# SSD chunk states: kept contiguous per chunk, with the recurrence as a chain of small operations

## The chip, the cores and the metric

The kernel runs on one core of a Trainium2 chip. The metric is the device time of one execution in microseconds; several runs are timed and their median is given.

## What is computed

One inference step of an encoder layer for a prompt of 1024 tokens and a sample of 32 tokens, width 1024, all in f32. After a conditioned RMSNorm an input projection (1024 to 4624 columns) feeds two groups: an RG-LRU group and an SSD group (16 heads of 64, two groups of B and C, state 128). Their outputs go through one output projection and a final RMSNorm. The change lies in the SSD group alone. Of the reference, cut:

```python
def ssd_scan(x, dA, Bm, Cm, s0, q):
    ...
    y_diag = jnp.einsum('bclgn,bcsgn,bgkcls,bcsgkp->bclgkp', Cm, Bm, Lm, x)   # inside a chunk
    states = jnp.einsum('bcsgn,bgkcs,bcsgkp->bcgkpn', Bm, decay_states, x)    # what a chunk adds
    ...
    new_states = ...    # state after chunk c = decay of chunk c * state before it + what it adds
    start_states, final = new_states[:, :-1], new_states[:, -1]
    y_off = jnp.einsum('bclgn,bcgkpn,bgkcl->bclgkp', Cm, start_states, jnp.exp(A_cs))
    return y_diag + y_off, final
```

(The reference writes the two products of `CB` and `y_diag` apart; they are drawn together here.) The kernel uses chunks of 128 tokens: chunks 0 to 7 are the prompt, whose state starts at zero, and chunk 8 is the sample, whose state starts from a given one. The final states of both are outputs.

## The kernel before

Channels lie on partitions, tokens on the free axis. The input projection takes a unit of 128 output channels at a time: `load_unit` fetches 512 KB of weights, ScalarE rounds them to the matmul's reduced f32 format (`whi`, L95), VectorE forms the remainder (`wlo`, L97), and TensorE does three products per piece (`pj`, L219 to L221) for three blocks of tokens (384, 384 and 290 columns).

The SSD stage is a loop of eight steps j (L685 to L712), two heads per step. A step has these parts:

- `ssd_tokens` (L558): transposes the inputs and scales them by dt, into `xdt` and `xw`.
- `ssd_decay` (L543): loads broadcast rows of decays `M` and `E` and scans `M` (L551).
- `ssd_states` (L573): for each of nine chunks one matmul adds up the chunk's contribution, [128 states, 128 = 2 heads x 64], into PSUM (`pd`, also called `dS` in the trace, L588): four chunks in one bank, four in the next, chunk 8 in a third. ScalarE copies the banks into the SBUF tile `dS` (L591), of shape [128, 128, 10]: for each of the 128 columns ten slots lie side by side, 0 to 7 for the chunks of the prompt, 8 for the sample's starting state (loaded into `st0`, copied by GpSimd, L579), 9 for the sample's chunk. ScalarE also spreads the decays of the chunks into a tile `dk` of the same shape (L580), with zeros in slots 0 and 8. One VectorE instruction then scans over all 1280 elements (L592): state = decay * state + contribution, where the zeros start the recurrence anew. GpSimd copies slots 7 and 9 into `sfin` (L595, L596), which is stored.
- `ssd_diag` (L600): the inside of each chunk, `yd` (L610), two matmuls per chunk, then `y` (L613).
- `ssd_off` (L617): for chunks 1 to 8 a matmul `yo` (L625) with the state before the chunk as weights, `dS[:, :, e]`, and `CT` as the moving operand; VectorE scales it by `E` (L628) and adds it to `y` (L629).

Between these, each step multiplies two units of the input projection and one of the conditioning (`ada_s`, `ada_row`, `ada_c`). The small products share four PSUM banks in turn, in the order in which the program asks for them (tag `g`); the projection has the other four. So the third piece of `yd` (chunk 8) takes over the bank in which the contributions of chunks 4 to 7 stood. `dS` has one buffer, so the state's parts of step j + 1 wait for the `yo` of step j.

In this stage the order of instructions on each engine is set by a list scheduler, which may put later projection matmuls between these parts. Each engine runs its own list in order; all DMAs are issued from SP's queue.

Of the kernel before, what the change touches and what calls it, by code (L numbers as in the profile page):

```python
# [8 lines left out]
F32 = mybir.dt.float32  # L9
F32R = mybir.dt.float32r  # L10
AF = mybir.ActivationFunctionType
OP = mybir.AluOpType
# [15 lines left out]

# columns of the packed per-channel parameters
P_NG, P_BADA, P_LCW, P_LCB = 0, 8, 32, 64  # L30
# [5 lines left out]

# The start. XLOAD: the order of the loads: x a piece of x, s a unit of w_ada (the scale's, then the
# shift's), w w_dt, B and C the first two tiles of the input projection's B columns. XP: pieces of x per
# block of tokens; SR: buffers for units of w_ada; POOL_K: the tiles of block 0 that GpSimd scales.
# PROG: the order on TensorE: r and R sum up a block's squares and spread its 1/rms, a and s multiply a  # L40
# unit of the scale's or the shift's, c turns finished rows into columns, d is a block of dt, p and q a
# k-tile of the two B tiles, W keeps the array's clock up where nothing is there to multiply.
WARM = 8
XP = (4, 2, 2)
SR = 6
POOL_K = (3, 5, 6)
XLOAD = "xxxxsxsCsBssswxsxsxssssssss"
PROG = ("WWWWWWWWWaWWWWWWraWRWcWaWWWWWWcWWWWqpaWWWaqcaqWp"
        "aWcqppapqcrqqRppdqprpqsqpRqppssqpqqpsssppqssdq")
# [8 lines left out]
def encoder_step(ctx: ExitStack, tc: tile.TileContext, a, o):  # L58
    nc = tc.nc
# [9 lines left out]
    dma = nc.sync.dma_start  # L69
# [3 lines left out]

    # ------------------------------------------------------------------ constants
    cT = const.tile([128, KT, 2], F32, name="cT")
# [9 lines left out]
    sel = const.tile([128, 32], F32, name="sel")  # L85

    # ------------------------------------------------------------------ weight units
    def fetch_unit(src):
        raw = wpool.tile([128, KT, 128], F32, name="wraw", tag="wraw", bufs=3)
        dma(raw, src)  # L90
        return raw
# [8 lines left out]
    def load_unit(src):  # L100
        return split_unit(fetch_unit(src))

    # ------------------------------------------------------------------ conditioning
    sc = const.tile([128, KT, 32], F32, name="sc")
# [3 lines left out]

    # four column tiles of the array share a unit's contraction; sel adds up their rows
    def ada_unit(raw, row, copy=nc.vector.tensor_copy):  # L110
        ps = pbank([128, 128], "ada_s")
        for kk in range(KT):
            q = slice(32 * (kk % 4), 32 * (kk % 4) + 32)
            nc.tensor.matmul(ps[q, :], lhsT=sc[:, kk, :], rhs=raw[:, kk, :], start=(kk < 4), stop=(kk >= 4))
        copy(row, ps)
# [6 lines left out]

    # 1 / rms of each token, tokens on partitions, from the sums over channel tiles of the squares; and
    # its spread over all partitions, tokens on the free axis
    def chunks(n):
        return [(c, t, min(128, n - t)) for c, t in enumerate(range(0, n, 128))]
# [26 lines left out]

    # ------------------------------------------------------------------ normalised input
    # channels on partitions; XB: a block's columns of x and its chunks of tokens
    XB = ((0, 384), (384, 384), (768, 288))
# [56 lines left out]

    # ------------------------------------------------------------------ input projection
    def mm_part(out, w, b, kk):
# [32 lines left out]

    # start: conditioning, h, dt and the first B tiles; what needs the shift comes last
    wdt = st.tile([128, KT, 16], F32, name="wdt")  # L250
# [7 lines left out]
    shift = st.tile([128, KT, 2], F32, name="shift")  # L258
    bk_b0, bk_b1 = {}, {}

    # rows 0..15 and 16..31: the products with the head and the tail of w_dt
    def dt_block(b):
# [9 lines left out]
    with tc.manual_schedule(engines={mybir.EngineType.SP, mybir.EngineType.PE}):  # L272
# [12 lines left out]

        # into the bank that the first of the k-tiles of block 1 overwrites
        def warm(n):
            for i in range(n):
                nc.tensor.matmul(bk_b0[1][:, 0:128], lhsT=ones[:, 0:128], rhs=ones[:, 0:128], start=True, stop=True)
# [47 lines left out]
        loads = list(XLOAD)  # L337
        for c in PROG:
            while loads and load_next():
                pass  # L340
            n = cnt[c]
            cnt[c] += 1
            b, k = divmod(n, KT)
# [15 lines left out]
            else:  # L359
                i = "pq".index(c)  # L360
# [8 lines left out]
        pd = dt_block(2)  # L369
# [5 lines left out]

    # tokens of each chunk on partitions, [chunk, head] on the free axis
    dtv = const.tile([128, 9, 16], F32, name="dtv")
    nc.gpsimd.memset(dtv, -1.0e4)
    pt = pbank([128, 9, 16], "dtT")
    for c in range(9):  # L380
        t0, L = (c * 128, 128) if c < 8 else (S0, TS)
# [7 lines left out]
    dec_bc = const.tile([128, 10, 16], F32, name="dec_bc")  # L389
# [5 lines left out]

    # ------------------------------------------------------------------ conv helper
    cso = const.tile([128, 20, 2, 3], F32, name="cso")
# [26 lines left out]

    # ------------------------------------------------------------------ SSD
    ss_cm = tc.tile_pool(name="ssdc", bufs=1)
    st_cm.__exit__(None, None, None)
    scn = ss_cm.__enter__()
    CT = scn.tile([128, 2, TW], F32, name="CT")
# [12 lines left out]
    tw = tw_cm.__enter__()  # L442
# [93 lines left out]
    for g in range(2):  # L536
        w = load_unit(a["w_in"][26 + g])
# [35 lines left out]
    def ssd_states(j, xw):  # L573
        g = j // 4
        st0 = tw.tile([128, 128], F32, name="st0", tag="st0", bufs=2)
        dma(st0, a["s_ssd"][j])
        dS = tw.tile([128, 128, 10], F32, name="dS", tag="dS", bufs=1)
        dk = tw.tile([128, 128, 10], F32, name="dk", tag="dk", bufs=1)
        nc.gpsimd.tensor_copy(dS[:, :, 8], st0)  # L579
        nc.scalar.copy(dk.rearrange("p (h q) c -> p h q c", h=2),  # L580
                       dec_bc[:, :, 2 * j:2 * j + 2].rearrange("p c h -> p h c")[:, :, None, :]
                       .to_broadcast([128, 2, 64, 10]))
        for cs_ in batches:
            n = len(cs_)
            pd = pbank([128, n, 128], "dS")
            for i, c in enumerate(cs_):
                L = chunk_cols(c)[1]
                nc.tensor.matmul(pd[:, i, :], lhsT=B_tm[0:L, g, c, :],  # L588
                                 rhs=xw[0:L, c].rearrange("p h q -> p (h q)"), start=True, stop=True)
            e0 = cs_[0] if cs_[0] < 8 else 9  # L590
            nc.scalar.copy(dS[:, :, e0:e0 + n].rearrange("p q c -> p c q"), pd)  # L591
        nc.vector.tensor_tensor_scan(dS.rearrange("p q c -> p (q c)"), dk.rearrange("p q c -> p (q c)"),  # L592
                                     dS.rearrange("p q c -> p (q c)"), 0.0, op0=OP.mult, op1=OP.add)
        sfin = tw.tile([128, 2, 128], F32, name="sfin", tag="sfin", bufs=2)
        nc.gpsimd.tensor_copy(sfin[:, 0, :], dS[:, :, 7])  # L595
        nc.gpsimd.tensor_copy(sfin[:, 1, :], dS[:, :, 9])  # L596
        dma(o["new_ssd"][j], sfin)
        return dS
# [18 lines left out]
    def ssd_off(j, y, stt, E):  # L617
        for cs_ in batches:
            prev = [c for c in cs_ if c > 0]
            t0, L = chunk_cols(prev[0])  # L620
            yo = pbank([128, len(prev), L], "yo")
            for i, c in enumerate(prev):
                c0, L = chunk_cols(c)
                e = c - 1 if c < 8 else 8
                nc.tensor.matmul(yo[:, i, :], lhsT=stt[:, :, e], rhs=CT[:, j // 4, c0:c0 + L], start=True, stop=True)  # L625
            sl = slice(t0, t0 + len(prev) * L)
            yf = yo.rearrange("p c l -> p (c l)")
            nc.vector.tensor_mul(yf, yf, E[:, sl])  # L628
            nc.vector.tensor_add(y[:, sl], y[:, sl], yf)  # L629
# [54 lines left out]
    stt = ssd_states(0, xw)  # L684
    for j in range(8):  # L685
# [23 lines left out]
        if j < 7:  # L709
            gate_row(j + 1)  # L710
            stt = ssd_states(j + 1, xw)
# [3 lines left out]

    # ------------------------------------------------------------------ RG-LRU
    with tc.using_default_side("right"):
# [55 lines left out]
    def lru_out(j, bg, h, sb=None):  # L773
# [5 lines left out]
    units = ([(0, d, 1) for d in range(KT)] + [(0, d, 0) for d in range(KT)]  # L779
             + [(b, d, h) for b in (1, 2) for d in range(KT) for h in (1, 0)])  # L780
    queue = [a["w_in"][u] for j in range(7) for u in (j + 1, j + 8)] + [a["w_in"][15]]
    queue += [a["w_out"][d, half] for (_, d, half) in units]
    split = {}
# [4 lines left out]

    # ScalarE keeps to this order so that functions of one table set stay together
    ins = lru_in(0, bx)  # L790
    with tc.manual_schedule(engines={mybir.EngineType.Activation}):
        prefetch(0)
        prefetch(1)
        for j in range(7):
# [4 lines left out]
            h = lru_scan(j, u, *gates, *decay)  # L799
# [6 lines left out]

    # ------------------------------------------------------------------ output projection
    # the last LRU step runs into it: the first block takes the SSD half of every output tile before the
    # LRU half, and each block's operands are split while the block before it is multiplied
    banks, parts, ots = {}, {}, {}  # L810
# [94 lines left out]
    with tc.manual_schedule(engines={mybir.EngineType.Activation, mybir.EngineType.DVE}):  # L905
# [18 lines left out]
        h = lru_scan(7, ins[0], *gates, *decay)  # L924
        prefetch(OUT0 + 4)
        for i in range(KT):
# [4 lines left out]
            if 1 <= i < 5:  # L931
                if i < 4:
                    prefetch(OUT0 + i + 4)
                for k in (2 * i - 2, 2 * i - 1):
                    last = lru_split(0, k)
# [5 lines left out]
    for i in range(KT, len(units)):  # L941
        b, d, half = units[i]
# [91 lines left out]
```

## Time and profile before

| | |
|---|---|
| median of three runs | 795.93 us (794.65 to 796.22) |
| profiled execution, span | 795.9 us |
| the SSD stage, 140 to 385 us | TensorE busy all of it |
| VectorE's scan of the states (L592) | 8 of 2.83 us |
| ScalarE's spreading of the decays (L580) | 8 of 2.48 us |
| ScalarE's copies of the contributions (L591) | 24, 18.2 us |
| GpSimd's copies of states (L579, L595, L596) | 24, 20.7 us |

The profile is of one execution. PE is TensorE's matmuls, PEld its weight loads, DVE VectorE, ACT ScalarE, POOL GpSimd, SP the engine that issues DMAs. A group's row gives the source line, engine, operation, output and inputs, shapes and count; behind the first bar busy time and the mean of one in ns, behind the second the engine's idle time just before it and what ended that. A row of the list by source line gives the least, median and greatest duration in ns. A row of the timeline gives start and length in us. Matmuls overlap, and their ends are modelled, so the distance between starts says what one costs. Where a matmul's form is 128*128, these are the weights' rows and columns.

### The profile page before, as it was taken

To read this page: it belongs to the slowest core of one execution; us is meant where nothing else is said; L and a number is where in the kernel's file an instruction comes from. 1 tells how busy PE (TensorE), PEld (TensorE's weight loads), DVE (VectorE), ACT (ScalarE), POOL (GpSimd) and SP (SyncE) were. 2 spreads that over 40 slices of the span, in tenths; PEclk is the share of its full clock that TensorE was granted. 3 is DMA by queue.
4 is the path that set the end of the run, shared out by engine and by line. 5 is a ranking of instruction groups with operands and counts; after the bars stand their busy time and mean duration, and the time that the engine had idled before them with its cause. 6 is when DMAs were issued, how large, how long until landed. Compare 5 with 4: busy or idle time off the path is not lost.

```text
span 795.9 us, 12952 instructions
## 1 busy us (share of the span) xinstructions
PE 775.1 (97%) x5230; PEld 751.6 (94%) x5230; DVE 531.8 (67%) x722; ACT 455.0 (57%) x636; POOL 103.7 (13%) x203
## 2 busy tenths in 40 slices
PE   8799999999999999999999999999999999999995
PEld 7678999999999999999999999999999999999994
DVE  3575956879678686876664665467567897644753
ACT  6553765656546475454379677967677755333330
POOL 3581211102111111011010111011101000000000
PEclk9899999999999999999999999999999999999998
DMA  9920214253334234342132111111133685644741
GB/s 336 393 82 13 77 36 137 88 156 123 124 108 120 104 96 155 118 120 81 47 100 74 56 43 45 45 50 56 34 104 129 203 266 168 222 149 149 241 128 67
DMA packets 39163, 96.31 MB, mean 121 GB/s; under 512 B 4536, under 2 KB 21184, under 8 KB 39104
## 3 DMA queue, kind: packets, MB, share of 16 engines
q1 hardware_dynamic: 39104, 95.50, 36.7%
q8 instruction: 41, 0.67, 0.4%
q14 instruction: 18, 0.15, 0.1%
HBM read 85.53 MB, written 9.95 MB: 120 GB/s over the span
## 4 chain that ended last, share of the span: by engine, by line
PE 87%; DVE 6%; DMA 3%; ACT 2%; issue 1%; POOL 1%; SPq 0%; POOLq 0%; DVEq 0%; ACTq 0%
PE pj L219 18%; PE pj L221 17%; PE pj L220 17%; PE mix L864 6%; PE mix L862 6%; PE mix L863 6%; PE yo L625 4%; PE yd L610 2%; PE dS L588 2%; DVE hb L211 2%; DMA sraw<-in_w_ada_dram 1%; DVE wlo L97 1%; PE xsT L567 1%; PE gt L746 1%; PE gt L748 1%
## 5 line engine op out<-in xcount | busy, mean ns | idle before, releaser
L219 PE MATMUL pj<-hb,whi 128*128 128x384 f32 (+1 forms) x864 | 286.7, 332 | 0.0
L220 PE MATMUL pj<-hb,whi 128*128 128x384 f32 (+1 forms) x864 | 282.8, 327 | 2.5 <-DVE hb L211 2.5
L221 PE MATMUL pj<-hb,wlo 128*128 128x384 f32 (+1 forms) x864 | 282.7, 327 | 1.3 <-POOL wlo L97 1.3
L220 PEld LDWEIGHTS pj<-hb,whi 128*128 128x128 f32 x864 | 164.0, 190 | 3.8 <-DVE hb L211 3.2
L219 PEld LDWEIGHTS pj<-hb,whi 128*128 128x128 f32 x864 | 163.5, 189 | 3.8 <-issue 3.2
L221 PEld LDWEIGHTS pj<-hb,wlo 128*128 128x128 f32 x864 | 164.2, 190 | 2.9 <-POOL wlo L97 1.6
L95 ACT CAST whi<-wraw 128x1024 fp32r<-128x1024 f32 x84 | 88.0, 1048 | 98.5 <-PE mix L863 69.3
L97 DVE TENSOR_TENSOR wlo<-wraw,whi 128x1024 fp32r<-128x1024 f32 x83 | 102.5, 1236 | 52.7 <-ACT whi L95 52.6
L864 PE MATMUL mix<-yt,wlo 128*128 128x324 f32 (+2 forms) x320 | 103.9, 326 | 0.5 <-DVE wlo L97 0.5
L862 PE MATMUL mix<-yt,whi 128*128 128x324 f32 (+2 forms) x320 | 104.1, 325 | 0.0
L863 PE MATMUL mix<-yt,whi 128*128 128x324 f32 (+2 forms) x320 | 103.7, 324 | 0.0
L419 DVE SCALAR_TENSOR_TENSOR u<-raw,par,u 128x1060 f32<-128x1060 f32 x60 | 79.6, 1327 | 0.8 <-ACT u L417 0.2
L864 PEld LDWEIGHTS mix<-yt,wlo 128*128 128x128 f32 x320 | 60.0, 188 | 0.9 <-DVE wlo L97 0.8
L862 PEld LDWEIGHTS mix<-yt,whi 128*128 128x128 f32 x320 | 60.1, 188 | 0.2
L863 PEld LDWEIGHTS mix<-yt,whi 128*128 128x128 f32 x320 | 60.0, 188 | 0.1
L238 ACT ACTIVATE raw<-pj,sb 128x384 f32<-128x384 f32 (+2 forms) x80 | 34.0, 477 | 29.3 <-PE pj L221 24.3
L592 DVE TENSOR_TENSOR_SCAN dS<-dk,dS 128x1280 f32<-128x1280 f32 x8 | 22.6, 2825 | 34.2 <-ACT dS L591 34.1
L551 DVE TENSOR_TENSOR_SCAN M<-M,mask 128x1060 f32<-128x1060 f32 x16 | 37.8, 2360 | 3.5 <-DMA M<-dA_d 3.5
L405 POOL COPY cso<-raw 128x3 f32<-128x3 f32 x20 | 15.5, 774 | 186.4 <-ACT raw L238 186.4
L881 DVE SCALAR_TENSOR_TENSOR ot<-mix,gate,xr 128x352 f32<-128x352 f32 (+3 forms) x32 | 14.8, 488 | 24.9 <-PE mix L864 21.4
L729 ACT CAST uh<-u 128x1060 fp32r<-128x1060 f32 x8 | 8.6, 1079 | 39.1 <-DVE u L419 39.1
L580 ACT COPY dk<-dec_bc 128x1280 f32<-128x1280 f32 x8 | 19.8, 2479 | 18.9 <-DVE dS L592 18.9
(232 smaller groups left out, 1151.9 us busy)
## 6 DMA issues: line engine op xcount, KB each, us to landing
wraw<-in_w_out_dram SPq DMA_DIRECT2D x48, 512.0 KB, 3.5
wraw<-in_w_in_dram SPq DMA_DIRECT2D x36, 512.0 KB, 3.6
M<-dA_d SPq DMA_DIRECT2D x16, 530.0 KB, 4.3
sraw<-in_w_ada_dram SPq DMA_DIRECT2D x16, 512.0 KB, 10.8
E<-E_d SPq DMA_DIRECT2D x16, 265.0 KB, 4.0
yz_d<-y SPq DMA_DIRECT2D x8, 530.0 KB, 3.9
wraw<-in_w_ada_dram SPq DMA_DIRECT2D x8, 512.0 KB, 3.5
x<-in_xh_dram SPq DMA_DIRECT2D x4, 384.0 KB, 4.6
```

The lines of the kernel that those rows point to most:

```text
L95: nc.scalar.copy(hi, raw)
L97: eng.tensor_sub(lo, raw, hi.bitcast(F32))
L219: nc.tensor.matmul(out, lhsT=hi[:, kk, :], rhs=hh, start=(kk == 0), stop=False)
L220: nc.tensor.matmul(out, lhsT=hi[:, kk, :], rhs=hl, start=False, stop=False)
L221: nc.tensor.matmul(out, lhsT=lo[:, kk, :], rhs=hh, start=False, stop=(kk == KT - 1))
L238: nc.scalar.activation(dst[0:P, off + d:off + d + e - s], banks[b][0:P, s:e], func, bias=sb[0:P, w:w + 1])
L419: nc.vector.scalar_tensor_tensor(u, raw[:, k:k + TW], wcol(k), u, op0=OP.mult, op1=OP.add)
L551: nc.vector.tensor_tensor_scan(M, M, mask, 0.0, op0=OP.add, op1=OP.mult)
L625: nc.tensor.matmul(yo[:, i, :], lhsT=stt[:, :, e], rhs=CT[:, j // 4, c0:c0 + L], start=True, stop=True)
L862: nc.tensor.matmul(ps, lhsT=w[0][:, k, :], rhs=yh, start=(half == 1 and k == 0), stop=False)
L863: nc.tensor.matmul(ps, lhsT=w[0][:, k, :], rhs=yl, start=False, stop=False)
L864: nc.tensor.matmul(ps, lhsT=w[1][:, k, :], rhs=yh, start=False, stop=(half == 0 and k == KT - 1))
```

## The change

`dS` becomes [128, 10, 128]: the 128 columns of a slot lie side by side. The sample's starting state is loaded straight into slot 8, and slots 7 and 9 are stored straight from `dS`; `st0`, `sfin`, `dk` and the GpSimd copies are gone. ScalarE copies only chunk 0's contribution. For every other chunk and each of the two heads one VectorE operation takes the slot before, a decay per partition and the contribution from PSUM, and writes the slot: sixteen operations of 128x64 per step, chained from chunk to chunk.

```diff
     def ssd_states(j, xw):
         g = j // 4
-        st0 = tw.tile([128, 128], F32, name="st0", tag="st0", bufs=2)
-        dma(st0, a["s_ssd"][j])
-        dS = tw.tile([128, 128, 10], F32, name="dS", tag="dS", bufs=1)
-        dk = tw.tile([128, 128, 10], F32, name="dk", tag="dk", bufs=1)
-        nc.gpsimd.tensor_copy(dS[:, :, 8], st0)
-        nc.scalar.copy(dk.rearrange("p (h q) c -> p h q c", h=2),
-                       dec_bc[:, :, 2 * j:2 * j + 2].rearrange("p c h -> p h c")[:, :, None, :]
-                       .to_broadcast([128, 2, 64, 10]))
+        dS = tw.tile([128, 10, 128], F32, name="dS", tag="dS", bufs=1)
+        dma(dS[:, 8, :], a["s_ssd"][j])
         for cs_ in batches:
...
-            e0 = cs_[0] if cs_[0] < 8 else 9
-            nc.scalar.copy(dS[:, :, e0:e0 + n].rearrange("p q c -> p c q"), pd)
-        nc.vector.tensor_tensor_scan(dS.rearrange("p q c -> p (q c)"), dk.rearrange("p q c -> p (q c)"),
-                                     dS.rearrange("p q c -> p (q c)"), 0.0, op0=OP.mult, op1=OP.add)
-        sfin = tw.tile([128, 2, 128], F32, name="sfin", tag="sfin", bufs=2)
-        nc.gpsimd.tensor_copy(sfin[:, 0, :], dS[:, :, 7])
-        nc.gpsimd.tensor_copy(sfin[:, 1, :], dS[:, :, 9])
-        dma(o["new_ssd"][j], sfin)
+            for i, c in enumerate(cs_):
+                if c == 0:
+                    nc.scalar.copy(dS[:, 0, :], pd[:, 0, :])
+                    continue
+                e = c if c < 8 else 9
+                for h in range(2):
+                    hs = slice(64 * h, 64 * h + 64)
+                    nc.vector.scalar_tensor_tensor(dS[:, e, hs], dS[:, e - 1, hs],
+                                                   dec_bc[:, e, 2 * j + h:2 * j + h + 1], pd[:, i, hs],
+                                                   op0=OP.mult, op1=OP.add)
+        dma(o["new_ssd"][j], dS[:, 7:10:2, :])
         return dS
...
-                nc.tensor.matmul(yo[:, i, :], lhsT=stt[:, :, e], rhs=CT[:, j // 4, c0:c0 + L], start=True, stop=True)
+                nc.tensor.matmul(yo[:, i, :], lhsT=stt[:, e, :], rhs=CT[:, j // 4, c0:c0 + L], start=True, stop=True)
```

The scheduler moves instructions. VectorE's list in step j = 5, before (`y` on L613, `yo` scaled on L628; the scan carries the name of its instruction class):

```order
292 L115 COPY ada_row<-ada_s 128x128
293 L592 SCALAR_TENSOR_TENSOR dS<-dk,dS 128x1280
294 L613 SCALAR_TENSOR_TENSOR y<-u,par,yd 128x512 x2
295 L613 SCALAR_TENSOR_TENSOR y<-u,par,yd 128x32
296 L628 TENSOR_TENSOR yo<-yo,E 128x384
```

The same place now (line numbers of the changed kernel, two less from here on):

```order
304 L115 COPY ada_row<-ada_s 128x128
305 L592 SCALAR_TENSOR_TENSOR dS<-dS,dec_bc 128x64 x10
306 L611 SCALAR_TENSOR_TENSOR y<-u,par,yd 128x512
307 L592 SCALAR_TENSOR_TENSOR dS<-dS,dec_bc 128x64 x6
308 L611 SCALAR_TENSOR_TENSOR y<-u,par,yd 128x512
309 L611 SCALAR_TENSOR_TENSOR y<-u,par,yd 128x32
310 L626 TENSOR_TENSOR yo<-yo,E 128x384
```

The chain stands where the scan stood, with the first piece of `y` in its midst: ten operations ahead of it (chunks 1 to 4 and the sample's), six behind it (chunks 5 to 7).

TensorE's list at the `yo` of step j = 5, before (`pj` is the projection, block 2 of it with 290 columns; each row of `yo` counts matmuls of the program):

```order
1268 L221 MATMUL pj_3039<-hb_84,wlo 128x384
1269 L625 MATMUL yo<-CT,dS 128x128 x3
1270 L219 MATMUL pj_3101<-hb_85,whi 128x290
1271 L220 MATMUL pj_3101<-hb_85,whi 128x290
1272 L221 MATMUL pj_3101<-hb_85,wlo 128x290
1273 L625 MATMUL yo<-CT,dS 128x128 x4
1274 L625 MATMUL yo<-CT,dS 128x32
```

And now:

```order
1260 L219 MATMUL pj_3075<-hb_84,whi 128x384
1261 L608 MATMUL yd<-M,xdt 64x128 x8
1262 L608 MATMUL yd<-M,xdt 64x32 x2
1263 L623 MATMUL yo<-CT,dS 128x128 x7
1264 L220 MATMUL pj_3075<-hb_84,whi 128x384
...
1274 L221 MATMUL pj_3137<-hb_85,wlo 128x290
1275 L623 MATMUL yo<-CT,dS 128x32
```

All of the prompt's `yo` now stands together, right behind the second and third piece of `yd`, and the sample's follows some projection matmuls later. Between the first piece of `yd` and the second stand seventeen projection matmuls where four stood, and none between the third and `yo` where nine stood.

## The prediction

> **What bounds the kernel now.** I read the page's list of engines first, then one stretch by engine, then the rows of the two lines that read the states.
>
> ```profile
> PE 775.1 (97%) x5230; PEld 751.6 (94%) x5230; DVE 531.8 (67%) x722; ACT 455.0 (57%) x636; POOL 103.7 (13%) x203
> DVE  3575956879678686876664665467567897644753
> core 0: us, PE busy (x) PEld busy (x) DVE busy (x) ACT busy (x) POOL busy (x), PEclk, DMA share, GB/s
> 140.00:385.00 245.00, 245.00 (x1762) 234.72 (x1761) 187.06 (x232) 132.80 (x154) 33.61 (x72) 1.00 0.36 114
> ```
>
> The last row is the SSD stage, where everything that changes lies. TensorE is busy for all of its 245 us, at a granted clock of 1.00; VectorE is busy for 76% of it, ScalarE for 54%, GpSimd for 14%. A busy TensorE may still be waiting inside, so I look at how far apart its matmuls start. The chain of waits runs through them (start, length, work), and the list by source line and the timeline show single ones. An f32 matmul of the program is two instructions in the trace.
>
> ```profile
> 154.47 3.49 PE yo L625 x16
> 177.41 3.53 PE yo L625 x16
> ...
> 380.37 1.30 PE yo L625 x6
> 382.07 2.18 PE yo L625 x10
> ```
>
> ```profile
> L625 PEld LDWEIGHTS yo<-CT,dS x128: 307/322/328, 154.1 to 383.8; 128*128 128x128 f32 x128
> L625 PE MATMUL yo<-CT,dS x128: 310/390/394, 154.3 to 383.9; 128*128 128x128 f32 x112, 128*128 128x32 f32 x16
> L588 PEld LDWEIGHTS dS<-xw,B_tm x144: 181/192/192, 143.6 to 375.0; 128*128 128x128 f32 x128, 32*128 32x128 f32 x16
> L588 PE MATMUL dS<-xw,B_tm x144: 270/275/377, 143.8 to 375.1; 128*128 128x128 f32 x128, 32*128 32x128 f32 x16
> ```
>
> ```profile
> 114.23 2.16 PE cb L527 x18
> ...
> 167.90 1.16 PE L588 MATMUL dS<-xw,B_tm 128*128 128x128 f32 x8
> 168.81 0.42 PE L219 MATMUL pj<-hb,whi 128*128 128x384 f32 x1
> ```
>
> Each of the eight steps spends 3.5 us on the sixteen instructions of `yo`: 0.22 us apiece, 27.9 us in all (3.49, 3.53, and about 3.48 for each of the six steps that have it in two pieces). `dS` is a matmul of the same size, 128x128 weights and 128 f32 columns, and eight of its instructions take 168.81 - 167.90 = 0.91 us, 0.114 apiece. What differs is the weights. `yo` loads `dS[:, :, e]`, one element in ten, 40 bytes apart; `dS` loads `B_tm`, which is contiguous. The load itself lasts 322 ns against 192, the matmul 390 against 275. The moving operand of `yo`, `CT`, is not the cause: `cb` moves it too, over contiguous weights, at 2.16 / 18 = 0.12 us apiece. So on the engine that bounds this stage, 0.1 us is lost 128 times.
>
> **The change part by part.** *TensorE.* After the change `yo` loads 128 contiguous elements per partition, as `dS` does. Fourteen full instructions at 0.114 are 1.60 us. The pair of chunk 8 moves only 32 columns, and no row has that over contiguous weights. The nearest pair moves 2 columns over 128x128 weights:
>
> ```profile
> 157.79 0.36 PE L120 MATMUL ada_c<-sel,ada_row 128*128 128x2 f32 x2
> 158.02 0.42 PE L221 MATMUL pj<-hb,wlo 128*128 128x384 f32 x1
> ```
>
> It takes 0.23 us for two. A quarter of 0.114, twice, is 0.06, the lower end. A group is then 1.66 to 1.83 us; I take 1.75, and 14.0 us for eight. The gain is 27.9 - 14.0 = 13.9 us. For the bounds: at 1.66 it is 14.6; with all sixteen at 0.122 (`dS` in whole steps, rows below) a group is 1.95 and the gain 12.3. The number of matmuls is the same, and `yo` stays in two pieces in the steps from j = 2; only step 0 gains a switch between kinds of matmul.
>
> [...]
>
> *VectorE.* One scan per step goes, sixteen small operations come: 128x64, one input in SBUF, one in PSUM, a scalar per partition. `y`, on L613, is that very form in two other sizes; the five rows behind it are two interleaved chains of small operations, each waiting for the one before the last, which is the new chain's pattern.
>
> ```profile
> L592 DVE TENSOR_TENSOR_SCAN dS<-dk,dS 128x1280 f32<-128x1280 f32 x8 | 22.6, 2825 | 34.2 <-ACT dS L591 34.1
> L613 DVE SCALAR_TENSOR_TENSOR y<-u,par,yd 128x512 f32<-128x512 f32 x16 | 11.1, 731 | 1.3 <-PE yd L610 1.3
> L613 DVE SCALAR_TENSOR_TENSOR y<-u,par,yd 128x32 f32<-128x32 f32 x8 | 1.9, 241 | 0.0
> L211 DVE SCALAR_TENSOR_TENSOR hb<-x,Acol,hb 128x32 fp32r<-128x32 f32 x8 | 3.1, 387 | 0.0
> ```
>
> ```profile
> 93.11 0.31 DVE L454 TENSOR_TENSOR dtbuf<-dtbuf 128x144 f32<-128x144 f32 x1
> 93.34 0.16 DVE L454 TENSOR_TENSOR lamn<-lamn 128x8 f32<-128x8 f32 x1
> 93.46 0.23 DVE L455 TENSOR_SCALAR dtbuf<-dtbuf 128x144 f32<-128x144 f32 x1
> 93.61 0.17 DVE L455 TENSOR_SCALAR lamn<-lamn 128x8 f32<-128x8 f32 x1
> 93.73 0.31 DVE L454 TENSOR_TENSOR dtbuf<-dtbuf 128x144 f32<-128x144 f32 x1
> ```
>
> (731 - 241) / 480 is 1.02 ns per element, so 64 elements take 241 + 33 = 274 ns. The four rows from 93.11 last 0.87 us together but fill 0.62, so neighbours overlap by 0.06: one operation per 0.21 us, sixteen in 3.4 us, where the scan took 2.83. The ends are 0.274 (no overlap) and 0.387, the dearest small operation of this instruction in the trace (L211); I take 0.21, because its rows have the same dependence. VectorE's load in the stage rises from 187.1 by 128 x 0.21 - 22.6 = 4.3 us to 191 us (214 with 0.387), out of 245 - 13.9 = 231: it doesn't become the bound.
>
> [...]
>
> *Whether the chain is in time.* This decides how much of 13.9 us is kept. Step j = 5 of before:
>
> ```profile
> 303.53 0.27 DVE L115 COPY ada_row<-ada_s 128x128 f32<-128x128 f32 x1
> 308.76 2.83 DVE L592 TENSOR_TENSOR_SCAN dS<-dk,dS 128x1280 f32<-128x1280 f32 x1 [4.96 <-ACT dS L591]
> ```
>
> ```profile
> 306.52 2.20 ACT L591 COPY dS<-dS 128x512 f32<-128x512 f32 x3 [2.31 <-PE dS L588]
> ```
>
> ```profile
> 305.38 2.36 PE L588 MATMUL dS<-xw,B_tm 128*128 128x128 f32 x18
> 307.67 1.09 PE L610 MATMUL yd<-M,xdt 128*64 128x128 f32 x16
> 308.69 0.44 PE L221 MATMUL pj<-hb,wlo 128*128 128x384 f32 x1
> ...
> 309.59 1.33 PE L610 MATMUL yd<-M,xdt 128*64 128x128 f32 x20
> 310.85 0.45 PE L219 MATMUL pj<-hb,whi 128*128 128x384 f32 x1
> ...
> 312.54 1.46 PE L625 MATMUL yo<-CT,dS 128*128 128x128 f32 x6
> ```
>
> ```profile
> L591 ACT COPY dS<-dS x24: 388/1065/1117, 145.3 to 376.0; 128x512 f32<-128x512 f32 x16, 128x128 f32<-128x128 f32 x8
> DMA to landing us min/median/max: 1.7/1.8/1.8
> ```
>
> (Here `dS` fills 18 instructions from 305.38 to 307.67, less than 0.13 apiece; in the chain of waits it is 2.20 us, 0.122.) VectorE stood idle for 4.96 us before the scan; now it begins as soon as chunk 0 is copied. That copy starts at 306.5 at the latest, where the copies of four chunks start now, and takes 0.39 (the smallest on L591): 306.9. Ten operations take 2.1 us, `y` of the first `yd` 0.73, the last six 1.3: done at 311.0. In the new order TensorE does `dS` and the first `yd` (to 308.69), seventeen projection matmuls (nine stand between the second `yd` and `yo` now, at (312.54 - 310.85) / 9 = 0.188 us; so to 311.9), the second `yd` (1.26), and `yo` at 313.1. The tightest need is the last piece of `yd`, which takes over the PSUM bank of chunks 4 to 7 at about 312.9: 1.9 us to spare, and 0.9 with operations of 0.274. I cost the new wait at nothing; what covers it are those seventeen matmuls and the second `yd`.
>
> *ScalarE and GpSimd* lose `dk`, two of three copies and all state copies; neither was the bound, so nothing is won there. *SP.* The state's load now goes straight into `dS`, so it waits for the `yo` of the step before, with `E` and the next weights queued behind it. `E` waits for VectorE to have read that same `yo` anyway, and the load lands in 1.8 us, while the `yo` of step 0 ends at 157.96 and the next `dS` starts at 167.90: nothing. The store of the states reads `dS` itself; it waits for the chain and stands ahead of both loads of `M`, which wait in turn for `yd`, which ends later.
>
> The sum against the profiled execution: 795.9 - 13.9 = 782.0 us. Its span equals the median of the runs shown (795.93), so nothing is added.
>
> **The rivals.**
>
> *Part is lost to a late chain* (0.12). If the operations cost 0.387, as on L211, the chain ends at 306.9 + 6.2 + 0.7 = 313.8, and TensorE waits 0.9 us per step: 7.2 us back, 789.2. For it: no row shows a 128x64 operation on this pattern. Against it: L613 has the form, at 241 ns for 32 elements.
>
> *Slower* (0.05), the same mechanism further on: TensorE waits at the last `yd` and at `yo` for longer than `yo` gained, 13.9 / 8 = 1.74 us per step. That decides from (312.9 + 1.74 - 306.9 - 0.73) / 16 = 0.44 us per operation; at 0.5, twice the 128x32 row, it is 1.0 us per step on the wrong side, 804. No row of this kind is that dear.
>
> [...]
>
> **How the numbers follow.** The forecast has 0.78. The range reaches from its upper bound of gain, 795.9 - 14.6 = 781.3, less the 1.3 us by which the fastest run shown lies under the median, to the late chain's 789.2: 780.0 to 789.2. The forecast alone is 780.0 to 784.9 (795.9 - 12.3, and the same 1.3 on the other side). 0.2% is 1.6 us, about what a measurement of this kernel can tell from no change (the runs lie 1.6 us apart). Faster: 0.78 + 0.12 = 0.90; same: 0.05; slower: 0.05.
>
> **What would show it.** Right: the loads of `yo` at about 192 ns and its matmuls at 275; groups of 1.75 us; the SSD stage 14 us shorter and the rest as before; the small operations at about 0.27 us, 0.21 apart; no wait of TensorE on VectorE's chain. Wrong: `yo` still 0.22 us apiece (the stride was not it), or gaps ahead of the last `yd` and of `yo` (the chain is late).

## The result and the profile after

The changed kernel takes 785.41 us (median of four runs, 784.74 to 786.8). The kernel before took 796.08 us beside it (794.65 to 796.75). The ratio is 0.9869, 95% interval 0.985 to 0.9888: 10.7 us faster. The forecast was 782.0 us, 13.9 us faster, in a range of 780.0 to 789.2. The direction and the mechanism hold; 3.2 us of the gain did not arrive. In an experiment's kernel one of four executions ran at a granted clock of 0.651 and took 1057.72 us; it is in no ratio.

The page of the changed kernel, with its engines and VectorE's row of slices, and the same stretch of the SSD stage by engine as before:

```profile
PE 761.6 (97%) x5230; PEld 737.0 (94%) x5230; DVE 534.5 (68%) x842; ACT 415.2 (53%) x609; POOL 78.0 (10%) x179
DVE  3575966798887787877475566546658897635643
```

```profile
140.00:385.00 245.00, 242.56 (x1827) 231.24 (x1826) 195.44 (x359) 98.33 (x134) 9.86 (x52) 1.00 0.37 117
```

TensorE was busy for 245.00 of 245.00 us in this stretch; now it is busy for 242.56, so 2.4 us of waits have appeared inside the stage that bounds the kernel. ScalarE and GpSimd lost what the change takes from them, 34 and 24 us in this stretch.

`yo`, by source line and in the chain of waits:

```profile
L623 PEld LDWEIGHTS yo<-CT,dS x128: 186/192/192, 151.7 to 372.0; 128*128 128x128 f32 x128
L623 PE MATMUL yo<-CT,dS x128: 190/275/377, 151.7 to 372.0; 128*128 128x128 f32 x112, 128*128 128x32 f32 x16
```

```profile
176.31 1.71 PE yo L623 x16
207.88 1.76 PE yo L623 x14
```

The load fell from 322 to 192 ns, the matmul from 390 to 275, a group from 3.5 us to 1.7 (the second row above lacks the sample's pair). Added up as distances between the starts of successive matmuls, all of `yo` went from 27.39 to 13.77 us: 13.6 saved.

The step j = 5 again, first TensorE, then VectorE and ScalarE:

```profile
296.18 2.36 PE L583 MATMUL dS<-xw,B_tm 128*128 128x128 f32 x18
298.46 1.09 PE L608 MATMUL yd<-M,xdt 128*64 128x128 f32 x16
302.68 1.33 PE L608 MATMUL yd<-M,xdt 128*64 128x128 f32 x20
303.94 1.83 PE L623 MATMUL yo<-CT,dS 128*128 128x128 f32 x14
```

```profile
297.56 2.06 DVE L592 SCALAR_TENSOR_TENSOR dS<-dS,dec_bc 128x64 f32<-128x64 f32 x10 [0.73 <-ACT dS L587]
299.61 0.75 DVE L611 SCALAR_TENSOR_TENSOR y<-u,par,yd 128x512 f32<-128x512 f32 x1
300.27 1.24 DVE L592 SCALAR_TENSOR_TENSOR dS<-dS,dec_bc 128x64 f32<-128x64 f32 x6
303.83 0.91 DVE L611 SCALAR_TENSOR_TENSOR y<-u,par,yd 128x512 f32<-128x512 f32 x2 [2.32 <-PE yd L608]
```

```profile
L592 DVE SCALAR_TENSOR_TENSOR dS<-dS,dec_bc x128: 258/273/281, 144.3 to 365.9; 128x64 f32<-128x64 f32 x128
  PEld yd L608: 0.2, 1
```

The chain is finished at 301.5, 1.2 us ahead of the second `yd`. VectorE then waits for TensorE (2.32 us) and not the other way round; in all eight steps TensorE waited for the chain once, for 0.2 us.

What TensorE does wait for in this stage, from its list of waits; none of these rows is in that of before:

```profile
PE xsT L567 <- ACT u L671: 1.1, 2, 0.7
PE xsT L567 <- DVE yo L626: 0.7, 1, 0.7
PE dS L583 <- DVE xdt L569: 0.6, 1, 0.6
```

They make 2.4 us, the idle time of the row of the stage. On the timeline such a wait looks like this (TensorE, the first of the four):

```profile
158.80 0.30 PE L220 MATMUL pj<-hb,whi 128*128 128x290 f32 x1
158.94 0.29 PE L221 MATMUL pj<-hb,wlo 128*128 128x290 f32 x1
159.95 0.74 PE L567 MATMUL xsT<-ident,u 128*128 128x128 f32 x5 [0.72 <-DVE yo L626]
```

`pj` instructions of this size start 0.14 us apart, and here 1.01 us pass. The row says 0.72, since a wait counts from the modelled end of the instruction before it. By starts the four gaps are 1.01, 0.87, 0.80 and 1.00 us, some 3.0 us more than those places cost without a wait. So about 13.6 - 3.0 = 10.6 us are left.

A second check is the distance from the first `bT`, the transposes at 92 us with which the matmuls ahead of the stage begin, to the first `gt` behind it. Before, then after:

```profile
L515 PE MATMUL bT<-ident,bt x18: 271/272/273, 92.5 to 97.5; 128*128 128x128 f32 x16, 128*32 128x128 f32 x2
L746 PE MATMUL gt<-uh,gh x48: 319/326/331, 395.8 to 586.0; 128*128 128x354 f32 x32, 128*128 128x352 f32 x16
```

```profile
L515 PE MATMUL bT<-ident,bt x18: 271/272/273, 91.3 to 96.3; 128*128 128x128 f32 x16, 128*32 128x128 f32 x2
L744 PE MATMUL gt<-uh,gh x48: 318/327/331, 384.1 to 573.9; 128*128 128x354 f32 x32, 128*128 128x352 f32 x16
```

That is 303.3 us before and 292.8 after: 10.5 us. I use this distance below and call it the stage's length. It is steadier than the time: `bT` itself starts between 90.1 and 92.6 us in all the profiled executions of this study but that slow one. One difference shows in the granted clock ahead of it; before, then after:

```profile
77.00:82.00 5.00, 5.00 (x28) 4.99 (x27) 4.24 (x7) 3.88 (x9) 4.24 (x8) 0.66 0.43 133
```

```profile
77.00:82.00 5.00, 5.00 (x40) 4.94 (x40) 4.37 (x9) 4.94 (x10) 3.88 (x7) 1.00 0.39 120
```

The profiled execution of before had a stretch at a lower clock there that the one of after had not. Further ahead it differs from execution to execution as well: over the first 50 us it is 0.90 in these two, and 0.97 and 0.93 in two of the experiments. So how much of the 1.2 us between the two `bT` is the clock's is open. Those 1.2 us lie ahead of the stage; the distance leaves them out.

### The profile page after: what moved, and what is told of

Read it like the earlier page. It is cut to its first block, busy times and chain, and to the rows that moved or that the text cites. A ratio compares the mean times of both kernels' runs of the same rounds, so it can differ in the third digit from the quotient of the medians.

```text
span 785.1 us, 13046 instructions
## 1 busy us (share of the span) xinstructions
PE 761.6 (97%) x5230; PEld 737.0 (94%) x5230; DVE 534.5 (68%) x842; ACT 415.2 (53%) x609; POOL 78.0 (10%) x179
## 4 chain that ended last, share of the span: by engine, by line
PE 80%; DVE 9%; DMA 5%; ACT 2%; issue 2%; POOL 1%; SPq 0%; POOLq 0%; DVEq 0%; ACTq 0%
PE pj L221 16%; PE pj L219 16%; PE pj L220 16%; PE mix L862 6%; PE mix L860 6%; PE mix L861 6%; PE yd L608 2%; PE dS L583 2%; DVE hb L211 2%; DMA M<-dA_d 2%; DVE wlo L97 1%; DMA sraw<-in_w_ada_dram 1%; PE yo L623 1%; DVE M L551 1%; PE gt L744 1%
## 5 line engine op out<-in xcount | busy, mean ns | idle before, releaser
L551 DVE TENSOR_TENSOR_SCAN M<-M,mask 128x1060 f32<-128x1060 f32 x16 | 37.8, 2363 | 11.8 <-DMA M<-dA_d 11.8
L405 POOL COPY cso<-raw 128x3 f32<-128x3 f32 x20 | 11.8, 590 | 195.9 <-ACT raw L238 195.9
L211 DVE SCALAR_TENSOR_TENSOR hb<-x,Acol,hb 128x384 fp32r<-128x384 f32 (+2 forms) x32 | 28.0, 925 | 3.8 <-ACT hb L210 3.8
L756 DVE SCALAR_TENSOR_TENSOR r<-a,r 128x1060 f32<-128x1060 f32 x8 | 10.1, 1264 | 28.2 <-ACT r L755 28.2
L554 ACT ACTIVATE M<-M 128x1060 f32<-128x1060 f32 x16 | 17.5, 1091 | 22.2 <-DVE M L551 20.3
```

The lines of the kernel that those rows point to most:

```text
L211: nc.vector.scalar_tensor_tensor(hb[b][:, k, 1, s:e], x[:, s:e], Acol[:, k, w:w + 1], hi.bitcast(F32), op0=OP.mult, op1=OP.subtract)
L551: nc.vector.tensor_tensor_scan(M, M, mask, 0.0, op0=OP.add, op1=OP.mult)
```

## The experiments

Three theories were tried. **A**: the gain is the layout that `yo` loads its weights from, 13.6 us, and what is missing is lost because VectorE's scan of `M` (L551) waits for its load. VectorE runs its list in order (in the step j = 5 above its rows from 297.56 us on start in the order of its list), so what stands behind the scan (the multiply on `yo`, which frees the bank that `xsT` needs, or the convolution that makes the input of `xsT`) is late for TensorE. **B**: the chain instead of the scan is the gain, not the layout. **C**: the 3 us are the price of VectorE's 120 more operations, wherever they stand.

The waits of VectorE for `M` in the two traces were A's ground, before and after:

```profile
DVE M L551 <- DMA M<-dA_d: 3.5, 4, 1.4
```

```profile
DVE M L551 <- DMA M<-dA_d: 11.8, 9, 2.4
```

And the first gap itself, on VectorE. The multiply at 159.72 is the one that `xsT` waited for; it stands behind a scan that waited 2.41 us for its load:

```profile
156.86 2.37 DVE L551 TENSOR_TENSOR_SCAN M<-M,mask 128x1060 f32<-128x1060 f32 x1 [2.41 <-DMA M<-dA_d]
159.14 0.66 DVE L627 TENSOR_TENSOR y<-y,yo 128x512 f32<-128x512 f32 x1
159.72 0.19 DVE L626 TENSOR_TENSOR yo<-yo,E 128x32 f32<-128x32 f32 x1
```

**The chain alone, in the old layout.**

```diff
-        dS = tw.tile([128, 10, 128], F32, name="dS", tag="dS", bufs=1)
+        dS = tw.tile([128, 128, 10], F32, name="dS", tag="dS", bufs=1)
...
-                    nc.vector.scalar_tensor_tensor(dS[:, e, hs], dS[:, e - 1, hs],
+                    nc.vector.scalar_tensor_tensor(dS[:, hs, e], dS[:, hs, e - 1],
...
-                nc.tensor.matmul(yo[:, i, :], lhsT=stt[:, e, :], rhs=CT[:, j // 4, c0:c0 + L], start=True, stop=True)
+                nc.tensor.matmul(yo[:, i, :], lhsT=stt[:, :, e], rhs=CT[:, j // 4, c0:c0 + L], start=True, stop=True)
```

(The diff is against the changed kernel; `st0`, `sfin` and GpSimd's copies are back as well.)

> The chain of the change, with the states interleaved as before (ten slots side by side, 40 bytes between the elements of a slot); the order on TensorE is that of the changed kernel. Theory A: yo stays at 0.21 to 0.22 us per instruction, loads of 322 ns; without the 13.6 us TensorE is slower at yo, so the late loads of M are hidden again; 796 us, up to 799 if the waits for M stay. Theory B: about 785, as the changed kernel.

Measured: 798.24 us, ratio to before 1.0024 (1.0012 to 1.0037). TensorE's order is that of the changed kernel, and `yo` is at its old price:

```profile
L628 PEld LDWEIGHTS yo<-CT,dS x128: 299/322/325, 151.8 to 383.4; 128*128 128x128 f32 x128
```

The chain by itself gains nothing; B falls. In this kernel TensorE has no wait in the stage, and VectorE waits for `M` no longer than before (3.5 us):

```profile
DVE M L551 <- DMA M<-dA_d: 2.9, 4, 1.3
```

With the layout alone, the next kernel, it waits 3.5 us as well. So the late `M` of the changed kernel needs both, the chain and the faster `yo`; the copies ahead of the chain, further below, show why.

**The layout alone, behind the old scan.** ScalarE copies nine slots of the scanned states into a contiguous tile, which `yo` reads.

```diff
+        dC = tw.tile([128, 10, 128], F32, name="dC", tag="dk", bufs=1)
+        nc.scalar.copy(dC[:, 0:9, :], dS[:, :, 0:9].rearrange("p q c -> p c q"))
-        return dS
+        return dC
...
-                nc.tensor.matmul(yo[:, i, :], lhsT=stt[:, :, e], rhs=CT[:, j // 4, c0:c0 + L], start=True, stop=True)
+                nc.tensor.matmul(yo[:, i, :], lhsT=stt[:, e, :], rhs=CT[:, j // 4, c0:c0 + L], start=True, stop=True)
```

(Against the kernel before.)

> The scan of before is kept with its interleaved states; ScalarE then copies slots 0 to 8 into a second tile where each slot's 128 elements lie side by side, and yo takes its weights from there. No chain. Theory A (the gain is the weights' layout alone, and what the change gave back comes from loads of M that start late): yo about 0.108 us per instruction, 13.6 us less than before; VectorE waits for M about as little as before (3.5 us), because the second piece of yd stands four projection matmuls behind the first as before; no wait of TensorE at xsT: 782.5 us. Theory B (the gain comes from replacing the scan, which ScalarE's copies held up): about 796, or above it by the 2 us copies.

Measured: 785.5 us, ratio 0.9859 (0.984 to 0.9878), so the layout carries the gain without any chain. Its trace comes from a further run:

> The scan kept, with ScalarE's copies of nine slots to a contiguous tile, for its trace. It was timed at 785.5 us where 782.5 had been expected. Theory A (a wait in another place than in the changed kernel): yo at 0.11 us per instruction, 13.6 us less in yo, and some 3 us of TensorE's gaps, which are not ahead of xsT by a late load of M but ahead of the last part of yo or behind it, since the scan and three copies of 2 us come one after the other there. Rival: no gaps, and yo slower than 0.11.

Measured: 785.7 us in the one run; `yo` 14.3 us by starts, 13.1 less than before; the stage's length 292.0, 11.3 less. So 1.8 us of the saving did not arrive, where A had expected some 3 us of gaps. TensorE has four waits in the stage, 0.96 us in all: 0.62 ahead of `ada_c` (0.95 by starts), 0.17 ahead of a projection matmul, and 0.09 and 0.07 ahead of a `yo`. None is ahead of `xsT`; that part of the expectation held. That the gaps would come to 3 us and stand at the last part of `yo` did not, and where the rest of the 1.8 us went is open.

**How far apart the weights may lie.** The chain's kernel with the slots interleaved in pairs (8 bytes from one weight to the next) and in fours (16 bytes).

```diff
-        dS = tw.tile([128, 10, 128], F32, name="dS", tag="dS", bufs=1)
+        dS = tw.tile([128, 5, 128, 2], F32, name="dS", tag="dS", bufs=1)
...
-                nc.tensor.matmul(yo[:, i, :], lhsT=stt[:, e, :], rhs=CT[:, j // 4, c0:c0 + L], start=True, stop=True)
+                nc.tensor.matmul(yo[:, i, :], lhsT=stt[:, e // 2, :, e % 2], rhs=CT[:, j // 4, c0:c0 + L], start=True, stop=True)
```

> The changed kernel with the slots in pairs: the elements of a slot lie 8 bytes apart (state load and store through GpSimd copies as before). If a weight load pays for each element that lies apart, whatever the distance: about 322 ns per load, 0.22 us per instruction of yo. If it pays in proportion to the distance up to some limit: in between, about 192 to 230 ns. If only distances over some size count: 192 ns and 0.11 us.

> The same with the slots in fours: 16 bytes between the elements of a slot. The same three readings; with a price in proportion to the distance it lies above the 8-byte case and below the 40-byte one (322 ns).

Measured, one run each beside a run of before of 797.13 us: 789.15 us at 8 bytes, 799.33 at 16. The rows of `yo` by source line, 8 bytes, then 16:

```profile
L628 PEld LDWEIGHTS yo<-CT,dS x128: 193/196/199, 153.1 to 374.1; 128*128 128x128 f32 x128
```

```profile
L628 PEld LDWEIGHTS yo<-CT,dS x128: 307/329/332, 152.9 to 385.1; 128*128 128x128 f32 x128
```

It is a step and not a slope: 192 ns at 4 bytes, 196 at 8, 329 at 16, 322 at 40. The step lies between 8 and 16 bytes; no distance between them was tried, and what makes it wasn't shown. TensorE's order is that of the changed kernel in both. (The one run at 8 bytes is 2.35 us above the changed kernel's profiled execution, 786.8; 1.3 us of that lie ahead of `bT`, and the stage's length, 293.6, is 0.8 more.)

**The scans of M behind the convolution.** In the changed kernel, both scans of `M` are issued behind the last operation of the convolution on VectorE.

```diff
-        if j < 7:
-            Ms, E = ssd_decay(j + 1)
         if j < 7:
             xs = ssd_x(j + 1, ssd_raw(banks, j + 1))
+            Ms, E = ssd_decay(j + 1, last_conv[0])
...
+                with tc.issue_after(after.ins):
+                    nc.vector.tensor_tensor_scan(M, M, mask, 0.0, op0=OP.add, op1=OP.mult)
```

> The changed kernel with one order laid down: on VectorE both scans of M of a step come behind the three operations of the convolution that makes the next x. M's loads stay as late as they are. Theory A (a late M holds up VectorE's list ahead of the convolution, and so the next x, its transposes on TensorE): the gaps ahead of xsT and dS go although M comes late: 782.4 us. Rival C (VectorE's load): 785.4, or worse, since the scans come later.

Measured: 785.51 us, ratio 0.9863 (0.9843 to 0.9884), by the time no different from the changed kernel. By the trace the stage's length is 291.6, 1.2 less. The two gaps behind `ACT u` are gone; the two of the first step, behind the multiply on `yo`, remain:

```profile
PE xsT L573 <- DVE yo L632: 0.7, 1, 0.7
PE dS L589 <- DVE xdt L575: 0.6, 1, 0.6
```

So A holds in the trace for the two gaps behind the convolution; by the time it is open.

**Four buffers of M.** `bufs=4` instead of 2 for the tag `M`.

> The changed kernel with four buffers for M instead of two, so that the loads of M of the next step don't wait for yd. Theory A: VectorE's waits for M (11.8 us in the changed kernel) fall to 3 us or less, TensorE's gaps ahead of xsT and dS (3.0 us) go: 782.4 us. Rival C (TensorE's gaps come from VectorE's greater load, the chain's 120 further operations, and not from M): as the changed kernel, 785.4.

Measured: 787.3 us (784.0 to 789.46), ratio 0.9882 (0.9861 to 0.9903); VectorE still waits 8.6 us, seven times, for `M`, and the stage's length is 292.4. The loads were not earlier in a step: on SP's queue they still stand behind the store of the states, which waits for the chain (35.9 us in the stage), and SP still waits for `yd` to issue them (13.0 us). TensorE still waits 1.3 us ahead of `xsT`, and 0.3 us once for the chain. The run took away less than it was meant to, and tells nothing apart.

**Copies ahead of the chain.** ScalarE copies every contribution into `dS` as it did before, and the chain runs in place.

```diff
+            e0 = cs_[0] if cs_[0] < 8 else 9
+            nc.scalar.copy(dS[:, e0:e0 + n, :], pd)
...
-                                                   dec_bc[:, e, 2 * j + h:2 * j + h + 1], pd[:, i, hs],
+                                                   dec_bc[:, e, 2 * j + h:2 * j + h + 1], dS[:, e, hs],
```

> ScalarE copies all contributions into the contiguous tile of states, as the scan's kernel did into its own, and the chain runs in place over them. The banks of PSUM come free by ScalarE's copies again, and the second piece of yd stands four projection matmuls behind the first again (seventeen in the changed kernel). Theory A (the yd that was put later holds the buffers of M, their loads come late, and VectorE's scan of M, with the convolution behind it, is late): VectorE waits about 3 us in all for the loads of M (11.8 in the changed kernel, 3.5 before), the gaps ahead of xsT are gone, yo stays at 0.11 us per instruction, and the time is 785.4 - 3.0 = 782.4 us. Rival C (the 3.0 us are the price of VectorE's 120 more operations, which this kernel has too): the gaps and the time stay, 785.4 us or a little more.

Measured: 785.61 us, ratio 0.9862 (0.9837 to 0.9886); the stage's length 291.6. The second `yd` is back four projection matmuls behind the first, as meant, and `yo` is at 0.10 us per instruction. But VectorE's wait for `M` did not fall:

```profile
DVE M L551 <- DMA M<-dA_d: 14.7, 8, 2.5
```

So A's expectation that `M` comes in time once `yd` is back is wrong. The gaps shrank to 0.60, 0.38 and 1.31 us by starts and did not go.

What makes `M` late shows in step j = 4, on TensorE, VectorE and SP. Before, then after:

```profile
270.77 2.36 PE L588 MATMUL dS<-xw,B_tm 128*128 128x128 f32 x18
274.22 2.82 DVE L592 TENSOR_TENSOR_SCAN dS<-dk,dS 128x1280 f32<-128x1280 f32 x1 [5.03 <-ACT dS L591]
276.34 0.33 SPq L550 DMA_DIRECT2D M<-dA_d  x1
281.68 2.36 DVE L551 TENSOR_TENSOR_SCAN M<-M,mask 128x1060 f32<-128x1060 f32 x1
```

```profile
261.62 2.36 PE L583 MATMUL dS<-xw,B_tm 128*128 128x128 f32 x18
269.48 0.80 SPq L550 DMA_DIRECT2D M<-dA_d  x2
273.40 2.37 DVE L551 TENSOR_TENSOR_SCAN M<-M,mask 128x1060 f32<-128x1060 f32 x1 [1.27 <-DMA M<-dA_d]
```

After, VectorE is ready for the scan at 273.40 - 1.27 = 272.13. The same for two more kernels, for the first load of `M` in this step, in us:

| | issued, from the first `dS` | VectorE ready, from the first `dS` | ready, from the issue | landed, from the issue |
|---|---|---|---|---|
| before | 5.6 | 10.9 | 5.3 | 3.4 |
| changed kernel | 7.9 | 10.5 | 2.6 | 3.9 |
| chain alone, old layout | 7.9 | 11.9 | 4.0 | 3.9 |
| copies ahead of the chain | 5.6 | 7.7 | 2.2 | 4.4 |

In the changed kernel the load is issued 2.3 us later in the step, and VectorE is ready hardly earlier. Putting `yd` back brings the load back, and VectorE with it: the load waits for `yd` to be done with the buffers of `M` (9.8 us of SP's waits in the changed kernel's stage), and VectorE's `y` waits for the same `yd`. What counts is VectorE's way from there to the scan. Before, the end of the scan of the states, three pieces of `y`, a multiply on `yo` and a `wlo`, with waits of 0.94 and 0.53 us, filled 5.3 us; now two pieces of `y` and three operations on `yo` fill 2.6. With the same list and `yo` at its old price VectorE waits 0.87 and 0.67 us for `yo`, and the 4.0 us are just enough. So `yo`'s own gain uncovers the load. This is read from four traces and wasn't tried by itself.

**Both edits.** The copies ahead of the chain, and the scans of `M` behind the convolution.

> The kernel with the copies ahead of the chain, and in addition both scans of M issued behind the convolution on VectorE from the second step on. Theory A: a late load of M can hold nothing but M itself, so the gaps ahead of xsT are gone by both edits, and the time is that of the copies alone, 782.4 us, or up to 0.5 us less. Rival C: 785.4 us.

Measured: 783.37 us, ratio 0.9842 (0.9819 to 0.9865); the stage's length 290.6, 2.2 less than the changed kernel's. One gap is left, 1.95 us by starts, in the first step again, behind the one scan of `M` in the stage that still waits and has work for TensorE behind it (`gate` frees the bank of `xsT`):

```profile
PE xsT L573 <- DVE gate L674: 1.7, 1, 1.7
```

**M earlier.** The changed kernel with four buffers of `M` and its loads on GpSimd's queue.

```diff
-            M = tw.tile([128, TW], F32, name="M", tag="M", bufs=2)
-            dma(M, dA_d[2 * j + h:2 * j + h + 1, :].to_broadcast([128, TW]))
+            M = tw.tile([128, TW], F32, name="M", tag="M", bufs=4)
+            nc.gpsimd.dma_start(M, dA_d[2 * j + h:2 * j + h + 1, :].to_broadcast([128, TW]))
```

> The changed kernel with four buffers of M instead of two, and M's loads issued from GpSimd's queue, where neither the store of the states nor yd stands ahead of them. The chain reads PSUM as in the changed kernel, and the second piece of yd stays sixteen or seventeen projection matmuls behind the first. Theory A (what was given back are loads of M that come late for VectorE): VectorE's wait for M falls from 11.8 us to under 2, all gaps of TensorE ahead of xsT and dS in the SSD stage are gone, the stage from the first xsT to the first gt takes 246.1 - 3.0 = 243.1 us, and the time is 782.4 us. Rival C (VectorE's work itself is late, whatever M does): the wait for M goes and the gaps stay, 246.1 us for the stage and 785.4 us.

Measured: 783.78 us, ratio 0.9855 (0.9832 to 0.9877); the stage's length 290.3, 2.5 less than the changed kernel's. One gap of 0.76 us is left. (From the first `xsT`, the distance that the expectation names, it is 239.8 us; but the first `xsT` starts 3.7 us later behind `bT` here, in another order, so the distance from `bT` is the fair one.) The loads still wait for `yd`, now on GpSimd's queue, 39.5 us in all. VectorE's wait for `M` fell to 7.7 us (six times, 3.4 of it ahead of the stage), not under 2: with four buffers the scans were put a whole step ahead of their use, and some of them still meet a load under way, but nearly nothing that TensorE needs soon stands behind them. So the wait itself need not cost anything; what is queued behind it decides.

**All of it.** Copies, scans behind the convolution, four buffers, GpSimd's queue.

> All of it together: ScalarE's copies of all contributions ahead of the chain, the scans of M behind the convolution, four buffers of M and its loads from GpSimd's queue. Theory A: the one gap left with the first two edits (1.95 us ahead of the second step's xsT, behind a scan that waits for M) goes too; the stage takes 243.8 - 1.8 = 242.0 us and the time is 783.4 - 1.8 = 781.6 us. Rival C: no change from 243.8 and 783.4 us.

Measured: 781.98 us (781.35 to 782.65), ratio 0.9821 (0.9803 to 0.9838). Its interval lies wholly below the changed kernel's (0.985 to 0.9888): it beats both kernels. TensorE's list of waits has no row of `xsT` or `dS` any more, and the stage runs from 91.4 to 380.3:

```profile
L517 PE MATMUL bT<-ident,bt x18: 270/272/273, 91.4 to 96.4; 128*128 128x128 f32 x16, 128*32 128x128 f32 x2
L750 PE MATMUL gt<-uh,gh x48: 318/327/331, 380.3 to 570.1; 128*128 128x354 f32 x32, 128*128 128x352 f32 x16
```

That is 288.9, 3.9 us less than the changed kernel's. From the first `xsT` it is 244.3, no less than the 243.8 of the two edits, where 242.0 had been expected; but the first `xsT` starts 2.0 us earlier behind `bT` here, and from `bT` the stage is 1.6 us shorter than with the two edits. Of the 3.9 us some 3.0 are the gaps. `yo`, `yd` and `dS` fill 12.8, 17.4 and 17.8 us by starts where they filled 13.8, 18.1 and 18.2, 2.2 less, and the projection, its gaps taken off, some 1.4 more; TensorE's order is another one here, and what of it saves the rest wasn't tried. The chain's 128 operations are all still there, at 0.272 us each, so C falls.

## Why the prediction was right and wrong

- **`yo` on TensorE: right.** By starts a group takes 13.77 / 8 = 1.72 us (1.75 forecast), the loads 192 ns and the matmuls 275, as named. The saving is 13.6 us for 13.9: the 27.9 us of before were lengths from the chain of waits, and by starts they are 27.39.
- **The layout as the cause: right.** The chain alone gains nothing, the layout alone 11 us. The load of the same 128x128 weights takes 196 ns at 8 bytes and 329 at 16. The 0.05 for an unchanged time is for a `yo` that stays at 0.22 us apiece whatever its layout; no run shows that: with contiguous weights the 128 cost 13.77 us in the changed kernel, 14.3 with the layout alone and 12.8 with all edits, 0.10 to 0.11 apiece.
- **The chain's price: right.** An operation lasts 0.273 us (0.274 forecast), and ten fill 2.06, so they start (2.06 - 0.273) / 9 = 0.20 apart (0.21 forecast). Neighbours overlap by 0.273 - 0.20 = 0.07 us (0.06 forecast).
- **The chain in time: right.** Set back by the 9.2 us by which this step's `dS` is earlier than before (305.38 to 296.18), the chain ends at 310.7 (311.0 forecast), the second `yd` starts at 311.9 (311.9) and `yo` at 313.1 (313.1). Both rivals of a late chain fall with it.
- **VectorE's load: right in size, wrong in what was drawn from it.** Its work in this operation rose by 26.0 - 22.6 = 3.4 us (4.3 forecast), and it isn't the bound. From the first `xsT` to the first `gt` VectorE is busy for 193.8 us before and 196.9 after; the row of 140 to 385 us rises by more, to 195.44, because it now ends with work from behind the stage. But "it doesn't become the bound" was argued from the sum over the stage, and the sum doesn't say whether single pieces of work come in time.
- **SP and `M`: the step that failed.** The prediction had it that the store of the states "waits for the chain and stands ahead of both loads of `M`, which wait in turn for `yd`, which ends later", and gave that no price and no reader. So much was right: in step j = 4 the load of `M` is issued 2.3 us later in the step. The reader is VectorE's scan of `M`, with work for TensorE behind it in the same list; it is ready 2.6 us after the issue where it was 5.3 before, and the load lands after 3.9. VectorE's 34.1 us of waits for ScalarE, on the row that the prediction quoted for the scan, fell to 4.6, and what VectorE would then be early for wasn't asked. The step cost about 3 us, the difference between 13.6 and 10.5. That these gaps come from what stands behind the scan of `M` is shown by the runs that moved the scans or their loads; that VectorE's shorter way from `yd` to the scan makes `M` late is read from the traces.
- **The range: partly luck.** The forecast by itself reached from 780.0 to 784.9, and 785.4 lies above that. It is inside the whole range because that one reaches on to the price of a late chain, and the chain was not late: what cost the 3 us had no term.
- **"The rest as before": right within the noise.** From the first `gt` to the end the two traces differ by under 1 us (0.24 to the last norm's product, the rest behind it). The span of 795.9 that the sum started from was not the median's: a device time is some 1.7 us longer than its span (786.8 and 785.1 for the profiled execution of after), and that execution had the stretch at a lower clock. The forecast figure isn't touched, since the median of before less 13.9 is 782.0 as well.

## What to carry to other kernels

Weights that are read often should lie contiguous, or close: here a load took 196 ns at 8 bytes from one to the next, 192 at 4, and 329 and 322 at 16 and 40; at 40 each instruction of `yo` cost 27.39 / 128 = 0.214 us by starts, where it cost 13.77 / 128 = 0.108 at 4. When a change takes an engine's waits away, or shortens work of another engine that it waits for, list what that engine does next, in its order, and ask for each whether its input is there that much earlier, and what stands behind it that the bounding engine needs. An engine that is 80% busy can still hold up one that is 99% busy, as VectorE (195.44 of 245 us) and TensorE (242.56) are in the changed kernel's stage, by a single instruction that waits at the wrong place in its list: the scan that waited 2.41 us for its load held up the multiply that `xsT` needed, and 1.01 us passed on TensorE in place of 0.14.

## What was not expected of the hardware

- The weight load's time has a step between 8 and 16 bytes from one weight to the next (196 and 329 ns); at 40 it is no longer (322).
- VectorE pays for the same stride much less: the chain's operation of 128x64 takes 0.273 us at 4 bytes, 0.274 at 8, 0.318 at 16 and 0.322 at 40.
- Without any edit to that part, the first `bT` starts up to 2.5 us earlier or later from one profiled execution to another, and the granted clock ahead of it differs: from 77 to 82 us it is 0.66 before and 1.00 after; from 50 to 80 us it is 0.97 before, 1.00 after and 0.94 in three of the experiments. How much of the difference is the clock's is open. For differences of 1 to 3 us, distances inside one trace decided more than the times.
